# Coarse-level values from DRAM copies, zeros stored early, a float32r mask and a new weave in a one-core mixer layer

## Chip, cores and metric

The kernel runs on one core of one Trainium2 chip. The metric is device time in microseconds (us) of one execution. The core's engines are TensorE (PE for its matmuls, PEld for its weight loads), VectorE (DVE), ScalarE (ACT), GpSimd (POOL) and SyncE (SP, which here only issues transfers). Each engine takes its instructions in a fixed order; they wait for each other by semaphores.

## The reference

One layer on 512 tokens of width 1024, in float32: a norm, one projection to 3112 columns, three mixers on slices of it, and one output projection with a residual.

```python
h = rmsnorm(x, norm_g[l]);  proj = jnp.matmul(h, w_in[l])
(gq, gk, gv, glr, gg, su, sg, nq, nkv, ngl, ng) = jnp.split(proj, IN_SPLITS, axis=-1)
y_gla = gla_mixer(gq, gk, gv, glr, gg, ...)   # 4 heads, decayed causal attention, state 32 x 64
y_s5  = s5_mixer(su, sg, ...)                 # 16 groups, complex diagonal recurrence, 64 states each
y_nsa = nsa_mixer(nq, nkv, ngl, ng, ...)      # 8 heads: compressed, block and window attention
x = x + jnp.matmul(jnp.concatenate([y_gla, y_s5, y_nsa], -1), w_out[l])
```

What of it bears on the change:

- In GLA the score of a query i and a key j <= i carries a decay for each channel between them. The kernel computes it in levels of 64, 32, 16, 8, 4, 2 and 1 tokens: at the level of size s, queries in an odd block of s tokens meet the keys and values of the even block just before it. So a level needs the values of every second block of s tokens.
- S5 is computed in chunks of 8 tokens. Within a chunk the output is the chunk's input times a block-Toeplitz matrix, whose other half is zero by causality.
- The two attention branches of NSA that remain (with 8 blocks and the 16 best chosen, every visible block is taken) are causal attention over 512 tokens, with a mask on the diagonal tile.

## The kernel before

**Arithmetic.** Most projections split both factors into a high and a low part of type float32r and add three products. `mm` (line 165) issues every matmul that is not a transpose, so most matmuls have that line and are told apart by their tiles. `load_part` (lines 228 to 230) brings a quarter of a weight group from DRAM on SP (`wr`), rounds it on ACT (`wh`) and subtracts on DVE (`wl`). `proj_t` and `proj_n` are the projections that use them.

**Streams.** The work is written as five streams: `p` (projections: values, compressed blocks, then the groups nq0, kv1, kv2, ng0, nq1, gg, sg, ng1), `g` (GLA: constants, decay, state, levels, output norm), `s` (S5: parameters, input matrix, scan, output matrix, output, gating), `n` (NSA: a small network on compressed blocks, then attention for two groups of heads) and `o` (output projection). Each stream is a chain of generators that yield between steps. `ORDER`, a string of 355 letters, says which stream takes its next step; `weave` walks it. A letter whose stream still waits for another one's stage does nothing. What a step emits comes behind everything emitted before it. That emission order is the instructions' priority; the tile framework's planner, which keeps a timeline of its own, turns it into the order of each engine's queue, and may put a later step's instructions ahead where it takes the earlier one's as not ready. Weight loads and the evacuation of projections are raised by a fixed priority.

**Memory.** Tiles come from slots in size classes (`al`, `fr`); a tile that takes over a slot waits for the last user of the tile before it. For a tile that a transfer fills, that wait is SP's or POOL's, and all later transfers of that queue stand behind it. Matmul outputs go to 8 banks handed out the same way.

**The places that the change touches.**

- `gla_v` ends with the store of the values `vv` to a DRAM tile `vd` (line 394, on POOL). In `gla_intra` each level reads its rows back as `ve`, 128 partitions by 2 halves by 256, with one SP transfer for each half (lines 501 to 505), and `smk` times `ve` is the level's output.
- `s5_out_weights` computes the Toeplitz matrix's columns `kt` (lines 716 to 723: a transpose of `kx` on PE, the diagonal `dk`, one addition). It clears a tile `zz` on POOL and sends it to the first 7 of 15 rows of a DRAM tile `kd`, sends `kt` to the other 8, and reads the matrix `tt` back with overlapping rows (lines 725 to 732, all three transfers on POOL). `s5_y` multiplies `tt` with the chunk inputs `u`, in four token steps; in each, products of `xs` with `hb` come first, then those of `u` with `tt`.
- `cmp_mlp` loads its first weights in eight steps of two SP transfers of 256 KB (`w`, line 968) and multiplies each with `bk`.
- `attn_score` adds the causal mask to the diagonal tile by a matmul of a bf16 identity with a bf16 mask (line 1145), behind two float32r matmuls of the query and key parts.

Of the kernel before, what the change touches and what calls it, by code (L numbers as in the profile page):

```python
# [18 lines left out]
T = 512  # L19
# [16 lines left out]
for _n, _w in SMALL:  # L36
# [4 lines left out]
JOB = (("j3", 2048, 2), ("j4", 4096, 2))  # L41
WMAX = 280
ORDER = (
    "sspsssppppppsssssssssoopogggpggggggggggppnppppppppopgnsnggpnpnngppppppppgsgsssssgggggnppgsggsggggsnn"
    "sgsgngsggggsngggggggnnsssnppppppnnnnnnpnpnnnnpnppnggggggppppgggggggggggpnnngpppnpnnpnnppppnnnnnngppn"
    "pppnpppnnppppooopnnnnnnnnnnnnnnnnnnonnonnnnnnnnnnnnnnnoonnnnnnoopnonnnonnnnnnnnnooooononoonnnnononnn"
    "onnnnoooonnnnonnooonooooooonnoooooonoonnoonooonnnnnnnnn"
)
WARM = 13
RING = 6  # L50
# [11 lines left out]
def kernel(ctx: ExitStack, tc: tile.TileContext, a: dict, out: bass.AP):  # L62
# [101 lines left out]
    def mm(o, l, r, start, stop, **kw):  # L164
        PE.matmul(o, lhsT=l, rhs=r, start=start, stop=stop, **kw)  # L165

    ident = const.tile([128, 128], F32, name="ident")
    identb = const.tile([128, 128], BF16, name="identb")
    maskneg = const.tile([128, 128], BF16, name="maskneg")
    ng = const.tile([128, NK], F32, name="ng")  # L170
    small = const.tile([128, SM_W], F32, name="small")
    rsc = const.tile([128, NT], F32, name="rsc")
# [182 lines left out]
        nc.gpsimd.dma_start(out=u.rearrange("p g n -> p (g n)"), in_=ud.rearrange("j (c g) n -> (j c) (g n)", c=16))  # L355

    def consts():
        N["w2b"] = al("w2b", (17, 128), keep=True)
        N["dm"] = al("dm", (128, NLV - 1, 128), F32R, keep=True)
        N["dm0"] = al("dm0", (128, 128), F32R, keep=True)  # L360
        dmr = al("dmr", (128, NLV - 1, 128))
        dmr0 = al("dmr0", (128, 128))
        N["cmask"] = const.tile([128, 7, 64], F32, name="cmask")
        N["bmask"] = const.tile([128, 256], F32, name="bmask")
        N["hind"] = al("hind", (128, 4), keep=True)
        N["bones"] = const.tile([128, 128], F32, name="bones")
        N["eps"] = const.tile([128, 1], F32, name="eps")
        nb = al("nb", (128, 128))
        nc.sync.dma_start(out=dmr, in_=a["dm"][:, 1:])
        nc.sync.dma_start(out=dmr0, in_=a["dm"][:, 0])  # L370
        nc.sync.dma_start(out=N["w2b"], in_=a["w2b"])
        nc.sync.dma_start(out=N["hind"], in_=a["hind"])
        nc.sync.dma_start(out=N["cmask"], in_=a["cmask"])
        nc.sync.dma_start(out=N["bmask"], in_=a["bmask"])
        nc.sync.dma_start(out=N["bones"], in_=a["bones"])
        nc.sync.dma_start(out=nb, in_=a["maskneg"])
        G.memset(N["eps"], EPS)
        S.activation(N["dm"], dmr, AF.Copy)
        S.activation(N["dm0"], dmr0, AF.Copy)
        V.tensor_copy(identb, ident)  # L380
        V.tensor_copy(maskneg, nb)


    def gla_v():
        N["vv"] = vv = al("vv", (128, NT, 256), keep=True)
        lr = N["lr"]
        g = group("v")
        for i in range(NT):
            with scope():
                ps = yield from proj_n(g, i, 272)  # L390
                evac(vv[:, i], ps[:, :256], i)
                evac(lr[:, i], ps[:, 256:272], i)
        vd = dram.tile([T, 256], F32, name="vd")
        nc.gpsimd.dma_start(out=vd.rearrange("(i p) e -> p i e", p=128), in_=vv)
        N["vd"] = vd

    def gla_decay():
        lr, w2b, dm, qT, kT = N["lr"], N["w2b"], N["dm"], N["qT"], N["kT"]
# [89 lines left out]
    def gla_intra():  # L488
        oT, vd, qT, kT = N["oT"], N["vd"], N["qT"], N["kT"]
        for lo, lv in ((-1, (0,)), (0, (1, 2)), (2, (3, 4)), (4, (5, 6))):  # L490
            with scope():
                nl = len(lv)
                exp_ = yield from gla_exp(lo, nl)
                ves = []
                for x, l in enumerate(lv):
                    s = LEVELS[l]
                    ex = exp_[:, x].rearrange("p (b z a s) -> p z b a s", b=4, z=2, s=s)
                    for z, src in ((0, qT), (1, kT)):
                        sv = src.rearrange("p (b a two s) -> p two b a s", b=4, two=2, s=s)[:, 1 - z]
                        V.tensor_tensor(ex[:, z], ex[:, z], sv, op=OP.mult)  # L500
                    ve = al("ve", (128, 2, 256))
                    for q in range(2):
                        nc.sync.dma_start(out=ve[:, q], in_=vd[256 * q:256 * q + 256].rearrange(
                            "(a two r) e -> two a r e", two=2, r=s)[0])
                    ves.append(ve)
                yield
                for h in range(4):
                    with scope():
                        hs = slice(32 * h, 32 * h + 32)
                        pg = bank()  # L510
                        pv = pg[:, :nl * 128].rearrange("p (l q t) -> p l q t", l=nl, q=2)
                        for x in range(nl):
                            for i in range(NT):
                                ex = exp_[hs, x]
                                mm(pv[64 * (i % 2):64 * (i % 2) + 64, x, i // 2],
                                   ex[:, i * 128 + 64:i * 128 + 128], ex[:, i * 128:i * 128 + 64], True, True)
                        sm_ = al("smk", (128, nl, 2, 64))
                        V.tensor_tensor(sm_, pv, N["cmask"][:, lv[0]:lv[0] + nl, None, :].to_broadcast([128, nl, 2, 64]),
                                        op=OP.mult)
                        yield  # L520
                        e = slice(64 * (h % 2), 64 * (h % 2) + 64)
                        for x, l in enumerate(lv):
                            s = LEVELS[l]
                            for i in range(NT):
                                b = slice(64 * (i % 2), 64 * (i % 2) + 64)
                                o = oT[i % 2].rearrange("p (h q a two s) -> p h q two a s", h=2, q=2, two=2, s=s)
                                mm(o[e, h // 2, i // 2, 1], ves[x][b, i // 2, h * 64:h * 64 + 64],
                                   sm_[b, x, i // 2].rearrange("p (a s) -> p a s", s=s), False,
                                   l == 6 and h >= 2 and i >= 2)
                        yield  # L530
        drop("dm", "dm0", "Lh", "Ll", "qT", "kT")
# [141 lines left out]
    def s5_out_weights():  # L673
# [48 lines left out]
                        eyed[:, None, :].to_broadcast([128, 16, 16]), op=OP.mult)  # L722
        V.tensor_tensor(kt, pk[:, :256], dk.rearrange("p a b -> p (a b)"), op=OP.add)
        fr(pk)
        kd = dram.tile([15, 16, 256], F32, name="kd")
        zz = al("zz", (112, 256))
        G.memset(zz, 0.0)
        nc.gpsimd.dma_start(out=kd[0:7].rearrange("l c x -> (l c) x"), in_=zz)
        nc.gpsimd.dma_start(out=kd[7:15].rearrange("l c x -> (l c) x"), in_=kt)
        N["tt"] = tt = al("tt", (128, 8, 256), keep=True)  # L730
        ka = kd[:]
# [399 lines left out]
    def attn_score(gx, i, pr, brs):  # L1131
        kA = N["kA"][gx]
        n, nb, b0 = (i + 1) * 128, len(brs), brs[0]
        h = gx * 4 + 2 * pr
        q = [N[f"qA{gx}"][:, 2 * pr + e, tok(i)] for e in range(2)]
        dn = al("dn2", (128, 2, nb), keep=True)
        p = al("p", (128, 2, T), keep=True)
        pv = p[:, :, :nb * n].rearrange("p e (b t) -> p e b t", b=nb)
        with scope():
            nm = al("nm", (128, 2, nb))  # L1140
            sv = [bank("ps")[:, :nb * n].rearrange("p (b t) -> p b t", b=nb) for _ in range(2)]
            for e in range(2):
                mm(sv[e], q[e], kA[:, 0, b0:b0 + nb, :n], True, False)
                mm(sv[e], q[e], kA[:, 1, b0:b0 + nb, :n], False, False)
                mm(sv[e][:, :, n - 128:], identb, maskneg[:, None, :].to_broadcast([128, nb, 128]), False, True)
            for e in range(2):
                V.tensor_reduce(nm[:, e], sv[e], axis=AX.X, op=OP.max, negate=True)  # L1147
            for e in range(2):
                for b in range(nb):
                    S.activation(pv[:, e, b], sv[e][:, b], AF.Exp, bias=nm[:, e, b:b + 1], accum_out=dn[:, e, b:b + 1])  # L1150
        V.reciprocal(dn, dn)
        V.tensor_tensor(dn, dn, gates[:, i].rearrange("p (h b) -> p h b", b=3)[:, h:h + 2, 1 + b0:1 + b0 + nb], op=OP.mult)  # L1152
        G.tensor_tensor(pv, pv, dn[:, :, :, None].to_broadcast([128, 2, nb, n]), op=OP.mult)  # L1153
        fr(dn)
        return p
# [66 lines left out]
def _prepare(inp):  # L1222
# [66 lines left out]
    a["bones"] = (t[:, None] // 64 == t[None, :] // 64).astype(np.float32) / 64.0  # L1289
    a["bmask"] = (t[:, None] // 32 == np.arange(256)[None, :] // 64).astype(np.float32)  # L1290
    a["hind"] = (t[:, None] // 32 == np.arange(4)[None, :]).astype(np.float32)
    a["eyed"] = (t[:, None] == np.arange(16)[None, :]).astype(np.float32)
    tok = np.arange(T).reshape(NT, 128).T
    vis = (np.arange(32) * 16 + 31)[None, None, :] <= tok[:, :, None]
# [30 lines left out]
```

## Time and profile before

| | |
|---|---|
| three runs | 377.41 us median, 374.65 to 380.54 |
| the profiled execution's own time | 376.93 us |
| its span, first to last instruction | 375.0 us |
| granted TensorE clock, mean over the span | 0.958 |
| TensorE busy with matmuls | 350.9 us (94%) |
| VectorE, ScalarE, GpSimd busy | 241.7, 163.7, 74.4 us |
| HBM traffic | 33.31 MB read, 3.39 MB written |

A row of the profile with busy times gives an engine's busy time and its instruction count. The row of the granted clock gives tenths of 2.4 GHz; the two levels are 2.4 GHz (1.0) and 1.2 GHz (0.5). Ends of matmuls are modelled and neighbours overlap, so the distance from start to start says more about a matmul's price than its duration. A wait is the idle time of an engine ahead of an instruction, with what ended it.

### The profile page before, as it was taken

The page shows a single profiled execution, that of the slowest core. Times are in us where ns is not written, and L with a number is a line of the kernel's source. Part 1 is how long each engine was busy: PE and PEld are TensorE (multiplying, and loading weights), DVE is VectorE, ACT ScalarE, POOL GpSimd, SP SyncE. Part 2 cuts the span into 40 slices and gives each one's busy share as a digit, 9 for nine tenths or more (in the row PEclk, how much of TensorE's full clock was granted, in tenths as well). Part 3 has the DMA queues.
Part 4 walks back from the last instruction along what each step waited for, and adds up shares of the span by engine and source line. Part 5 has one row for each costly group of instructions (what it writes and reads, how often), then busy time and mean ns, then how long its engine had stood idle before and what let it go on. Part 6 is the DMA issues. An engine that isn't in the chain of part 4 may idle for free.

```text
span 375.0 us, 6778 instructions
## 1 busy us (share of the span) xinstructions
PE 350.9 (94%) x2620; PEld 277.7 (74%) x2620; DVE 241.7 (64%) x502; ACT 163.7 (44%) x355; POOL 74.4 (20%) x75
## 2 busy tenths in 40 slices
PE   7999997999995995999999999899989997999996
PEld 3889977999884663679877867687666885677785
DVE  2749979985995220356674876985898776564332
ACT  3773441447743010353532436844876254632110
POOL 0000420100010000000130122463576243541000
PEclk9999998999999576999999999999999998799999
DMA  6995563344258023651324020020332024110022
GB/s 188 318 353 164 133 207 92 93 142 138 61 152 281 14 73 88 227 144 33 101 77 142 12 47 0 3 59 28 113 114 86 0 73 152 56 59 2 34 94 97
DMA packets 26509, 39.81 MB, mean 106 GB/s; under 512 B 2981, under 2 KB 15534, under 8 KB 26478
## 3 DMA queue, kind: packets, MB, share of 16 engines
q1 hardware_dynamic: 25150, 35.94, 31.7%
q0 software_dynamic: 1328, 3.46, 3.1%
q8 instruction: 20, 0.33, 0.4%
q14 instruction: 11, 0.09, 0.1%
HBM read 33.31 MB, written 3.39 MB: 98 GB/s over the span
## 4 chain that ended last, share of the span: by engine, by line
PE 65%; DVE 14%; DMA 11%; ACT 5%; issue 3%; POOL 1%; SPq 0%; ACTq 0%; DVEq 0%; POOLq 0%
PE pp L165 28%; PE pt L165 17%; PE ps L165 14%; PE pt L1172 4%; DMA w<-in_w_dram 2%; DMA tt<-kd 2%; DMA wor<-in_w_out_dram 2%; DVE wl L230 2%; DMA xr<-in_xT_dram 1%; DMA dmr<-in_dm_dram 1%; DMA wr<-in_w_nq_dram 1%; DMA kd<-kt 1%; DVE wol L1076 1%; ACT wh L229 1%; DVE nm L1147 1%
## 5 line engine op out<-in xcount | busy, mean ns | idle before, releaser
L165 PE MATMUL pp<-wl,xh 128*128 128x256 f32 (+2 forms) x160 | 46.3, 291 | 2.4 <-DVE wl L230 2.4
L230 DVE TENSOR_TENSOR wl<-wr,wh 128x512 fp32r<-128x512 f32 (+2 forms) x48 | 35.0, 741 | 20.6 <-ACT wh L229 18.9
L1153 POOL TENSOR_TENSOR p<-p,dn 128x1024 f32<-128x1024 f32 (+2 forms) x24 | 39.4, 1640 | 44.6 <-DVE dn L1152 30.5
L165 PE MATMUL pp<-wh,xh 128*128 128x256 f32 (+2 forms) x160 | 46.4, 292 | 0.6 <-ACT qr L280 0.6
L165 PE MATMUL pp<-wh,xl 128*128 128x256 f32 (+2 forms) x160 | 46.5, 292 | 0.0
L229 ACT ACTIVATE wh<-wr 128x512 fp32r<-128x512 f32 (+2 forms) x48 | 30.2, 635 | 29.4 <-PE pp L165 12.5
L1150 ACT ACTIVATE p<-ps,nm 128x512 f32<-128x512 f32 (+3 forms) x64 | 33.1, 528 | 16.5 <-DVE nm L1147 14.7
L165 PEld LDWEIGHTS pp<-wl,xh 128*128 128x128 f32 x160 | 30.8, 193 | 2.9 <-DVE wl L230 2.6
L165 PE MATMUL pp<-xh,wh 128*128 128x512 f32 x80 | 32.1, 401 | 0.6 <-DVE sgt L285 0.6
L1147 DVE TENSOR_REDUCE nm<-ps 128x1 f32<-128x512 f32 (+3 forms) x48 | 27.8, 593 | 7.4 <-PE ps L165 7.3
L165 PEld LDWEIGHTS pp<-wh,xh 128*128 128x128 f32 x160 | 30.8, 193 | 1.9 <-ACT qr L280 0.8
L165 PE MATMUL pp<-xl,wh 128*128 128x512 f32 x80 | 31.8, 398 | 0.0
L165 PE MATMUL ps<-kA,qA 128*128 128x512 f32 (+2 forms) x96 | 29.8, 405 | 2.0 <-ACT p L1150 1.2
L165 PE MATMUL pp<-xh,wl 128*128 128x512 f32 x80 | 31.6, 398 | 0.0
L165 PEld LDWEIGHTS pp<-wh,xl 128*128 128x128 f32 x160 | 30.8, 193 | 1.0 <-issue 0.8
L165 PE MATMUL pt<-pT,kvr 128*64 128x128 f32 x320 | 28.0, 288 | 2.2 <-DVE pT L1176 2.2
L1172 PE MATMUL pt<-ident,p 128*128 128x128 f32 x160 | 25.3, 287 | 0.5 <-POOL p L1153 0.5
L165 PEld LDWEIGHTS pt<-pT,kvr 128*64 128x64 f32 x320 | 19.8, 140 | 7.2 <-DVE pT L1176 2.6
L1172 PEld LDWEIGHTS pt<-ident,p 128*128 128x128 f32 x160 | 17.8, 143 | 5.8 <-issue 4.3
L1178 ACT ACTIVATE pT<-pt 128x512 f32<-128x512 f32 (+1 forms) x22 | 12.3, 560 | 18.5 <-PE pt L1172 18.4
L165 PEld LDWEIGHTS ps<-kA,qA 128*128 128x128 f32 x96 | 15.6, 197 | 4.8 <-ACT p L1150 1.7
L165 PEld LDWEIGHTS pp<-xh,wh 128*128 128x128 f32 x80 | 15.1, 188 | 3.9 <-DVE sgt L285 0.8
(381 smaller groups left out, 760.5 us busy)
## 6 DMA issues: line engine op xcount, KB each, us to landing
w<-in_w_dram SPq DMA_DIRECT2D x16, 256.0 KB, 4.5
wor<-in_w_out_dram SPq DMA_DIRECT2D x16, 256.0 KB, 2.8
xr<-in_xT_dram SPq DMA_DIRECT2D x8, 256.0 KB, 5.0
xn<-in_xn_dram SPq DMA_DIRECT2D x4, 512.0 KB, 8.3
wr<-in_w_kv_dram SPq DMA_DIRECT2D x8, 256.0 KB, 3.3
wr<-in_w_nq_dram SPq DMA_DIRECT2D x8, 256.0 KB
wr<-in_w_ng_dram SPq DMA_DIRECT2D x8, 256.0 KB, 3.7
opart<-in_xn_dram SPq DMA_DIRECT2D x4, 512.0 KB
```

The source lines that it names most:

```text
L165: PE.matmul(o, lhsT=l, rhs=r, start=start, stop=stop, **kw)
L229: S.activation(hs[qt][:, :, :w], r[:, :, :w], AF.Copy)
L230: V.tensor_tensor(ls[qt][:, :, :w], r[:, :, :w], hs[qt][:, :, :w].bitcast(F32), op=OP.subtract)
L1076: (V if hf else G).tensor_tensor(wol[k][:, c], r, woh[k][:, c].bitcast(F32), op=OP.subtract)
L1147: V.tensor_reduce(nm[:, e], sv[e], axis=AX.X, op=OP.max, negate=True)
L1150: S.activation(pv[:, e, b], sv[e][:, b], AF.Exp, bias=nm[:, e, b:b + 1], accum_out=dn[:, e, b:b + 1])
L1153: G.tensor_tensor(pv, pv, dn[:, :, :, None].to_broadcast([128, 2, nb, n]), op=OP.mult)
L1172: PE.transpose(pb[:, tok(x_)], p[:, e, c:c + 128], ident)
L1178: S.activation(pt[:, :w], pb[:, :w], AF.Copy)
```

## The change

Four edits:

- **Values.** Behind the store of `vd` come three further stores on POOL: one that writes the even blocks of 64 tokens to a DRAM tile of half the size, two that do so for blocks of 32. The levels of 64 and 32 then read `ve` in one SP transfer each; the level of 1 is also written as one transfer, from `vd`. The other four keep two.
- **Zeros.** `kd` is made in `consts`, and its first 7 rows are filled there by a transfer from a DRAM input of zeros. `zz`, its clearing and its transfer in `s5_out_weights` go.
- **Mask.** The identity and the mask for `attn_score` become float32r instead of bf16, in the same 48 matmuls.
- **Weave.** `ORDER` is another string of 355 letters, with differences nearly everywhere.

Where the two strings put some steps, found by walking them (letters counted from 0):

| step | before | after |
|---|---|---|
| `s5_params`, first step | 0 | 1 |
| store of the values | 28 | 28 |
| `w1` loads and products 0 to 4 of `cmp_mlp` | 53, 55, 59, 61, 62 | 54, 56, 59, 60, 61 |
| `kt`, `kd` and the load of `tt` | 54 | 55 |
| `ve` of the level of 64 | 72 | 71 |
| four token steps of `s5_y` | 73, 75, 76, 77 | 69, 70, 72, 73 |
| `w1` 5 to 7 | 85, 98, 99 | 82, 104, 105 |
| projection kv1 | 65 to 86 | 68 to 92 |
| projection kv2 | 126 to 140 | 94 to 147 |
| projection ng0 | 147 to 158 | 156 to 165 |
| projection nq1 | 159 to 186 | 166 to 189 |

```diff
-    identb = const.tile([128, 128], BF16, name="identb")
-    maskneg = const.tile([128, 128], BF16, name="maskneg")
+    identr = const.tile([128, 128], F32R, name="identr")
+    maskneg = const.tile([128, 128], F32R, name="maskneg")
...
     def consts():
+        N["kd"] = kd = dram.tile([15, 16, 256], F32, name="kd")
+        nc.gpsimd.dma_start(out=kd[0:7].rearrange("l c x -> (l c) x"), in_=a["zero"])
...
-        N["vd"] = vd
+        N["vd"] = {0: vd}
+        for s in (64, 32):
+            N["vd"][s] = half = dram.tile([T // 2, 256], F32, name=f"vd{s}")
+            hv = half.rearrange("(i h r) e -> h r i e", i=NT, r=s)
+            for h in range(64 // s):
+                nc.gpsimd.dma_start(out=hv[h], in_=vv[2 * s * h:2 * s * h + s])
...
-                    for q in range(2):
-                        nc.sync.dma_start(out=ve[:, q], in_=vd[256 * q:256 * q + 256].rearrange(
-                            "(a two r) e -> two a r e", two=2, r=s)[0])
+                    if s in vd:
+                        nc.sync.dma_start(out=ve, in_=vd[s].rearrange("(q p) e -> p q e", q=2))
+                    elif s == 1:
+                        nc.sync.dma_start(out=ve, in_=vd[0].rearrange("(q p two) e -> two p q e", q=2, two=2)[0])
+                    else:
+                        for q in range(2):
+                            nc.sync.dma_start(out=ve[:, q], in_=vd[0][256 * q:256 * q + 256].rearrange(
+                                "(a two r) e -> two a r e", two=2, r=s)[0])
...
-        kd = dram.tile([15, 16, 256], F32, name="kd")
-        zz = al("zz", (112, 256))
-        G.memset(zz, 0.0)
-        nc.gpsimd.dma_start(out=kd[0:7].rearrange("l c x -> (l c) x"), in_=zz)
+        kd = N["kd"]
...
-                mm(sv[e][:, :, n - 128:], identb, maskneg[:, None, :].to_broadcast([128, nb, 128]), False, True)
+                mm(sv[e][:, :, n - 128:], identr, maskneg[:, None, :].to_broadcast([128, nb, 128]), False, True)
```

## Rows read from the trace of the kernel before

**Rows 1.** The page's busy totals, its 40 slices of the span for TensorE, and the granted clock by slice.

```profile
PE 350.9 (94%) x2620; PEld 277.7 (74%) x2620; DVE 241.7 (64%) x502; ACT 163.7 (44%) x355; POOL 74.4 (20%) x75
...
PE   7999997999995995999999999899989997999996
...
PEclk9999998999999576999999999999999998799999
```

**Rows 2.** The longest waits of TensorE: what waited, for what, us in total, times, the longest.

```profile
PE ps L165 <- DMA tt<-kd: 4.4, 1, 4.4
PE pt L165 <- DMA w<-in_w_dram: 4.3, 1, 4.3
```

**Rows 3.** Busy time of each engine in chosen stretches: stretch, its length, busy us and instructions of PE, PEld, DVE, ACT and POOL, granted clock, share of the DMA engines' time, GB/s.

```profile
66.00:117.60 51.60, 50.84 (x443) 47.05 (x441) 44.85 (x98) 29.63 (x53) 3.13 (x6) 1.00 0.44 130
...
121.56:135.21 13.65, 13.16 (x64) 9.06 (x66) 3.24 (x8) 0.60 (x1) 0.00 (x0) 0.50 0.04 15
135.21:142.04 6.83, 5.51 (x52) 3.92 (x48) 1.57 (x3) 1.78 (x3) 0.00 (x0) 1.00 0.56 153
...
142.04:148.86 6.82, 3.84 (x17) 2.20 (x19) 0.00 (x0) 0.00 (x0) 0.00 (x0) 0.50 0.24 60
150.00:230.00 80.00, 79.19 (x807) 60.73 (x804) 51.15 (x106) 31.30 (x57) 10.91 (x13) 1.00 0.33 92
230.00:316.00 86.00, 81.24 (x594) 61.00 (x592) 66.77 (x122) 52.22 (x135) 41.67 (x28) 1.00 0.21 62
```

**Rows 4.** The order of POOL's instructions from 40 to 120 us: start, us, line, operation, out<-in, count, and in brackets the idle time before and what ended it.

```profile
44.13 0.76 POOL L394 DMA_DIRECT2D vd<-vv  x1
52.71 2.11 POOL L949 DMA_DIRECT2D aT<-tm  x4 [7.82 <-DVE fr L635]
...
107.89 0.31 POOL L727 MEMSET zz<- 112x256 f32 x1 [41.12 <-DVE Ll L191]
108.50 0.57 POOL L728 DMA_DIRECT2D kd<-zz  x1 [0.30 <-POOL zz L727]
109.06 0.57 POOL L729 DMA_DIRECT2D kd<-kt  x1
114.43 0.92 POOL L732 DMA_DIRECT2D tt<-kd  x1 [4.80 <-DMA kd<-kt]
```

**Rows 5.** From VectorE's order in time, the instruction that makes `kt`; and, from the instructions on the tile `kx`, the transposes that `kt` reads (duration ns min/median/max, first and last start).

```profile
108.35 0.42 DVE L723 TENSOR_TENSOR kt<-ps,dk 128x256 f32<-128x256 f32 x1
...
L716 PE MATMUL ps<-ident,kx x2: 273/301/329, 96.5 to 96.7; 128*128 128x128 f32 x2
```

**Rows 6.** TensorE's matmuls in order of time around the two waits.

```profile
115.65 0.39 PE L165 MATMUL pp<-xh,wl 128*128 128x512 f32 x1
...
122.05 0.69 PE L165 MATMUL ps<-tt,u 128*64 128x128 f32 x4 [4.44 <-DMA tt<-kd]
...
145.02 1.11 PE L165 MATMUL pt<-w,bk 128*64 128x256 f32 x2 [4.30 <-DMA w<-in_w_dram]
...
159.59 0.28 PE L165 MATMUL pp<-wh,xh 128*128 128x256 f32 x1
159.71 0.28 PE L165 MATMUL pp<-wl,xh 128*128 128x256 f32 x1
```

**Rows 7.** SP's transfers in order of time between 115 and 151 us, and what SP waited longest for ahead of a `ve` transfer.

```profile
117.70 0.41 SPq L228 DMA_DIRECT2D wr<-in_w_sg_dram  x1
134.50 1.19 SPq L503 DMA_DIRECT2D ve<-vd  x2
135.86 2.63 SPq L968 DMA_DIRECT2D w<-in_w_dram  x2
...
SPq L503 <- PE pt L165: 19.8, 3, 16.3
```

**Rows 8.** Transfers: count, KB of each, median us from issue to landing.

```profile
tt<-kd POOLq DMA_DIRECT2D x1, 1024.0 KB, 7.6
...
aT<-tm POOLq DMA_DIRECT2D x8, 64.0 KB, 2.0
...
kd<-kt POOLq DMA_DIRECT2D x1, 128.0 KB, 4.8
```

**Rows 9.** The mask among its neighbours: TensorE's matmuls and weight loads in order of time.

```profile
280.83 0.63 PE L165 MATMUL ps<-kA,qA 128*128 128x512 f32 x2
...
281.30 0.10 PEld L165 LDWEIGHTS <-identb 128*128 128x128 bf16 x1 [0.27 <-issue]
281.30 0.23 PE L165 MATMUL ps<-maskneg,identb 128*128 128x128 bf16 x1
...
281.34 0.71 PE L165 MATMUL ps<-kA,qA 128*128 128x512 f32 x2
...
281.90 0.23 PE L165 MATMUL ps<-maskneg,identb 128*128 128x128 bf16 x1
```

**Rows 10.** Weight loads by form: count, busy us, mean ns, idle before and what ended it.

```profile
L165 PEld LDWEIGHTS ps<-kA,qA 128*128 128x128 f32 x96 | 15.6, 197 | 4.8 <-ACT p L1150 1.7 <-issue 1.2 <-DVE kA L923 0.9
...
L165 PEld LDWEIGHTS <-identb 128*128 128x128 bf16 x48 | 4.7, 98 | 9.9 <-issue 9.4
```

**Rows 11.** Two float32r matmuls on 128 columns that follow each other, in a stretch where the clock was 0.5.

```profile
128.00 0.42 PE L165 MATMUL ps<-dm,Ll 128*128 128x128 f32 x1
128.21 0.41 PE L165 MATMUL ps<-dm,Lh 128*128 128x128 f32 x1
```

More of the change, by code (lines that the diff above doesn't have):

```diff
@@ L43 @@
 ORDER = (
[L44 to L47, printed above, removed]
+    "psssssssppspsposspssposggpogpoopoognpgpppgggppppggggggnsnggnnngppppppssgssgsgpgppsnspppgggggppppsggg"
+    "gggsnnsgsngsggggsngpgggsnnnnnnnnnnnsgsggpppnnnpppgggggggpggpnnppgppppppgggggggnpnngnnnnpnppnppppnnnn"
+    "nnnnpppppppgpnnppnnnnnpnnnnnnnnnnnnnnnnnnonnonnnnnnnonnnnoooonnooonnnnnopoooonnnooonnnnnoonnnnnnnnnn"
+    "nnnnnonnnoooooonononnoooonoonooononnonoonoononnnnnonnon"
 )
@@ L379, in consts @@
         S.activation(N["dm0"], dmr0, AF.Copy)
-        V.tensor_copy(identb, ident)
+        V.tensor_copy(identr, ident)
         V.tensor_copy(maskneg, nb)
@@ L1291, in _prepare @@
     a["hind"] = (t[:, None] // 32 == np.arange(4)[None, :]).astype(np.float32)
+    a["zero"] = np.zeros((112, 256), np.float32)
     a["eyed"] = (t[:, None] == np.arange(16)[None, :]).astype(np.float32)
```

## The prediction, made before the change was run

> **What bounds the kernel now.** I read the page's totals first: TensorE is busy for 350.9 of 375.0 us, and no other engine comes near [rows 1]. So a change can win only TensorE's own work, its idle time (some 24 us) and the time that it runs at the half clock. The slices show where these lie: ones of 5 to 7 tenths in the clock's row stand at about 120 to 150 us, and the busy row dips there too [rows 1]. Then the waits of TensorE: the two longest are one of 4.4 us for the transfer of `tt` and one of 4.3 us for the first weights `w` of `cmp_mlp`; no other reaches 2.5 us [rows 2].
>
> Then the stretches. From 66 to 117.6 us TensorE is busy for 50.84 of 51.6 us at the full clock, with VectorE at 44.85. Behind the first wait the clock is 0.5 from 121.56 to 135.21 us, with 13.16 us of matmuls, and behind the second from 142.04 to 148.86 with 3.84 us [rows 3]. Work at half clock takes twice as long, so half of those matmul times is lost: 6.6 and 1.9 us. The bill of the two waits is 4.4 + 6.6 + 4.3 + 1.9 = 17.2 us. After 150 us little is left: 0.8 us idle in 150 to 230 and 4.8 in 230 to 316 [rows 3].
>
> Why do the waits stand there? `kt` is added at 108.35 us, its transfer is issued at 109.06, the load of `tt` at 114.43 after a wait of 4.80 for that transfer [rows 4, 5], and TensorE goes on at 122.05 [rows 6]. That is 13.3 us from the end of `kt` (108.77) to its use. In the meantime TensorE used up the projection ng0 until 115.65 us; the next projection in its queue is nq1 at 159.59 [rows 6]. So the queue's own order leaves nothing to cover the end of the chain. The second wait is SP's doing: after 117.70 it issues nothing until 134.50, where it was held 16.3 us by TensorE for a `ve` transfer, and two loads of `w` stand behind that at 135.86 [rows 7].
>
> **The change part by part**, against the profiled execution's 376.93 us (span 375.0 and 1.9 around it; the median of the runs is 0.5 above).
>
> *Zeros.* The clearing of `zz` (107.89) and its transfer (108.50) go; they kept POOL until 109.06, and `kt` was ready at 108.77 [rows 4, 5]. That is 0.3 us on the chain to `tt`, from the rows. The transfer of `kt` (128 KB) landed in 4.8 us beside the zeros; the nearest one alone, `aT` with 64 KB, in 2.0 [rows 8]. So the gain is between nothing (the chain is covered anyway) and 0.3 + 2.8 = 3.1 us; I take 0.5, near the issue time, because the load of `tt` itself (1 MB, 7.6 us) is unchanged. The early transfer of zeros costs nothing: POOL, busy for 20% of the span [rows 1], stands idle most of the time, and 112 KB are some 0.3% of what is read. Without that cover it would be one issue of 0.57 us on POOL [rows 4]. The Trainium skill ("DMA: Bandwidth & Descriptors", Anatomy of one DMA) gives a transfer on this path a fixed 2 us and bytes over 436 GB/s, so an estimate of 2.3 us for `kt` against the row's 4.8; by that rule the chain would be 2.5 us shorter and the sum lower by as much.
>
> *Values.* SP issues 11 `ve` transfers instead of 14. SP's issue takes 0.6 us of each (1.19 for two [rows 7]), 1.8 us in all, and TensorE never waited for `ve` among its longest waits [rows 2]; cover is SP's idle time, so nothing on the path. The three further stores stand on POOL behind 44.13 at 0.76 each, 2.3 us; behind them on POOL are the `aT` transfers, which wait for VectorE until 52.71 [rows 4], so they are covered by that idle time of 7.8 us. Without it, the compressed blocks would come 2.3 us later.
>
> *Mask.* Two pairs of the same matmuls tell its price: the first pair starts at 280.83, its mask at 281.30, so 0.47 for two; from the mask to the next pair is 0.04, and that pair takes until 281.90, so 0.56 for two. One mask matmul costs 0.04 + 0.09 = 0.13 us [rows 9]: the load of the bf16 identity begins only when the matmuls before it have run (48 loads, 9.4 us of such idle time [rows 10]). In float32r at 128 columns the nearest row is 0.21 us from start to start at clock 0.5, so about 0.105 at 1.0 [rows 11]. That is 0.02 less each, 1.0 us for 48. The ends: half the 0.12 of a 256-column one [rows 6], so 0.07 less each, a gain of 3.4 us; or the longer load shows in full, 197 against 98 ns [rows 10], a loss of 4.8 us. I take the gain of 1.0, as float32r loads before the 512-column matmuls are hidden already.
> A rule speaks against this edit. The Trainium skill ("TensorE: Matmul & The Clock Gate", Weight-path perf modes) says that the fast weight load needs 128 weights that aren't FP32. The trace agrees on the load (98 against 197 ns); by the rule alone the 4.8 us would be lost.
>
> *Weave.* The direct edits come to 1.5 us; the rest hangs on the new order. The letters decide little by themselves: ng0 has letters 147 to 158 and ran before `s5_y` with 73. So I weigh what the new walk does to the two waits. For `tt`: between the `kt` step and the first token step of `s5_y` stood 9 half projections, now 5. Each is 12 matmuls of 0.12 us [rows 6], so 5.8 us less by the letters: the first wait is not helped. For `w`: the `ve` load of the level of 64 stood ahead of all four token steps of `s5_y`, with TensorE's wait among them; now two of them and the same five `w` loads stand ahead of it, so SP is less likely to hold `w` behind a slot that TensorE frees late. And projections kv1 and kv2 now have letters behind `s5_y`. I take it that the second wait goes with its clock, 4.3 + 1.9 = 6.2 us, and that the first stays. Ends: 17.2 us (both go) and nothing, or a loss (below).
>
> Sum: 376.9 - 0.5 - 1.0 - 6.2 = 369.2 on the profiled scale, 369.7 beside the median.
>
> **Rivals.**
> - *Neither wait goes.* The planner put TensorE's work in an order of its own, and SP still stands in line for `ve`. Then only the direct 1.5 us are left: 375.9. For it: both waits come from transfers that landed later than the queue's order allowed for, and the letters around them moved by few places. Against: the string differs nearly everywhere.
> - *Both go.* Were `kt` added earlier, `tt` would be there at 117.6: the transposes it reads were done at 97 us, 11 us before it [rows 5], so there is room for the 4.4. Then 376.9 - 1.5 - 17.2 = 358.2, or 358.7 beside the median. Against: VectorE was busy up to there [rows 3], and the change does nothing to its work.
> - *Slower: the cover before `tt` shrinks.* If the 5.8 us fewer of projections show in full, TensorE waits 10.2 us for `tt`, and the stretch from 135.21 to 142.04 (5.51 us of matmuls [rows 3]) runs at half clock too, 5.5 us more; the second wait is absorbed in part. 376.9 - 1.5 + 5.8 + 5.5 = 386.7, less some 2 of the second wait: 385. It decides once more than about 1.5 us of the cover is lost without the `w` wait going. For it: the letters. Against: TensorE had no cover left from 115.65 on in any case.
> - *The mask's load shows.* A loss of 4.8 where I have a gain of 1.0: 369.7 + 5.8 = 375.5. Against: the idle time of 9.4 us ahead of the bf16 loads [rows 10], which float32r loads don't have.
>
> **How the numbers follow.** The second wait goes: 0.34, between 365 and 374 with the ends of the mask and of the zeros. Neither goes: 0.24. Both go: 0.20. Slower: 0.18. The mask's load: 0.04. A measurement of this kernel tells about 2% from no change, so faster means under 369.9. Faster: half of 0.34, and 0.20: 0.37. Slower by over 2% (above 385.0) would need all of the fourth case and it ends just there; as its price is rough and other places of the order can fail likewise, I keep 0.18. Within 2%: 0.17 + 0.24 + 0.04 = 0.45. The likeliest case gives 369.7, and its middle lies at the bound, so that "within" leads. The range goes from 359 (both) to 381: what lies above is the slower case, under 2 in 10.
>
> **What would show it.** The waits of TensorE: `w` gone from them, `tt` still at 3 to 5 us, with a clock of 0.5 for one stretch instead of two between 115 and 150 us. In SP's order no gap of 16 us ahead of `ve`. For the zeros: no clearing at POOL, and `kt`'s transfer right behind the addition. For the mask: idle time ahead of the identity's loads well under 9.4 us, and about 0.1 us from a mask to the next start. It is wrong if TensorE's longest wait is a new one, after 150 us above all, or if `kt` is added at another time than 108 us by more than 3 us: then the order of VectorE moved and my sum misses its main term.

## The result, and the profile after the change

The changed kernel takes 363.64 us (median of 4 runs, 361.91 to 364.86) where the kernel before takes 377.35 (374.65 to 380.54): a ratio of 0.966, 95% interval 0.959 to 0.973. The forecast was 369.7 within 359 to 381; "faster", which came, had a chance of 0.37 there, behind 0.45 for "within 2%". Some runs of a kernel are slower than its others by some per cent, so medians here are over every run and ratios over the faster ones alone, of which two kernels below had too few.

The page after, beside [rows 1]: busy totals, TensorE's slices and the granted clock.

```profile
PE 342.8 (95%) x2620; PEld 279.9 (77%) x2620; DVE 238.4 (66%) x502; ACT 163.4 (45%) x355; POOL 77.2 (21%) x77
...
PE   6999997979999599999999999899999999899996
...
PEclk9899999989999858999999999999999999999999
```

The dip at 120 to 150 us is shorter, and the 7 and 8 that stood near the end of the clock's row are gone. TensorE's longest waits after, beside [rows 2]:

```profile
PE ps L165 <- DMA tt<-kd: 4.0, 1, 4.0
PE pp L165 <- DVE wl L230: 3.8, 2, 2.7
PE pt L165 <- ACT xh L296: 2.2, 1, 2.2
PE pt L165 <- DVE pT L1185: 1.9, 3, 1.0
```

The wait on `w` is gone, the one on `tt` is there, and none other is above 3 us in one piece. The stretches after, beside [rows 3]; the columns are the same:

```profile
66.00:121.20 55.20, 52.51 (x447) 48.97 (x445) 45.97 (x102) 28.65 (x51) 3.54 (x6) 0.97 0.42 124
121.20:125.42 4.22, 0.21 (x4) 0.00 (x0) 0.00 (x0) 0.00 (x0) 0.00 (x0) 0.84 0.77 251
124.04:137.69 13.65, 12.27 (x60) 8.53 (x60) 3.21 (x7) 1.82 (x3) 0.00 (x0) 0.50 0.13 42
137.69:150.00 12.31, 12.31 (x105) 8.11 (x104) 2.75 (x5) 2.25 (x4) 0.00 (x0) 1.00 0.73 216
150.00:230.00 80.00, 79.06 (x827) 62.73 (x825) 53.73 (x112) 37.80 (x69) 11.25 (x13) 1.00 0.28 77
230.00:318.00 88.00, 85.61 (x638) 68.78 (x638) 70.06 (x138) 53.21 (x151) 50.29 (x33) 1.00 0.27 79
```

Of the two half-clock stretches in this part the one behind the `tt` wait is left (12.27 us of matmuls, 13.16 before); from 137.69 us TensorE is busy without a gap at the full clock. POOL's order after, beside [rows 4]:

```profile
46.61 1.74 POOL L402 DMA_DIRECT2D vd<-vv  x3
56.88 2.11 POOL L958 DMA_DIRECT2D aT<-tm  x4 [8.54 <-DVE tm L953]
...
112.46 0.56 POOL L738 DMA_DIRECT2D kd<-kt  x1 [44.12 <-DVE on L558]
116.67 0.91 POOL L741 DMA_DIRECT2D tt<-kd  x1 [3.65 <-DVE nfs L187]
```

The copies cost POOL 1.74 us, covered by its 8.54 us of idle time. The zeros are gone from the chain. `kt` is now added at 111.74 us and the first product of `tt` starts at 125.42, so the chain takes 13.68 us; it took 13.70 [rows 5, 6]. SP's order after, beside [rows 7]:

```profile
127.19 0.37 SPq L228 DMA_DIRECT2D wr<-in_w_sg_dram  x1
137.87 0.37 SPq L510 DMA_DIRECT2D ve<-vd  x1
138.83 0.81 SPq L977 DMA_DIRECT2D w<-in_w_dram  x2
140.79 0.33 SPq L971 DMA_DIRECT2D w<-in_w2c_dram  x1
```

SP is still held for 10 us ahead of `ve`, and `w` still stands behind it. But two `w` transfers are issued in 0.81 us, not 2.63. That small row is the trail that the experiments follow.

### The profile page after: what moved, and what is told of

The parts are those of the page before. It is cut to its first block, busy times and chain, and to the rows that moved or that the text cites. A ratio compares the mean times of both kernels' runs of the same rounds, so it can differ in the third digit from the quotient of the medians.

```text
span 361.8 us, 6782 instructions
## 1 busy us (share of the span) xinstructions
PE 342.8 (95%) x2620; PEld 279.9 (77%) x2620; DVE 238.4 (66%) x502; ACT 163.4 (45%) x355; POOL 77.2 (21%) x77
## 4 chain that ended last, share of the span: by engine, by line
PE 54%; DVE 5%; DMA 4%; ACT 4%; issue 1%; ACTq 0%
PE pp L165 25%; PE pt L165 14%; PE ps L165 10%; PE pt L1181 4%; DMA tt<-kd 2%; DMA wor<-in_w_out_dram 2%; DVE nm L1156 1%; ACT p L1159 1%; DVE wol L1085 1%; ACT woh L1084 1%; ACT pT L1187 1%; DVE dn L1161 1%; DVE pT L1185 0%; DVE mixf L574 0%; DVE sgt L288 0%
## 5 line engine op out<-in xcount | busy, mean ns | idle before, releaser
L165 PE MATMUL ps<-kA,qA 128*128 128x512 f32 (+2 forms) x96 | 28.5, 389 | 1.1 <-ACT p L1159 1.1
L165 PE MATMUL pt<-pT,kvr 128*64 128x128 f32 x320 | 26.6, 281 | 1.9 <-DVE pT L1185 1.9
L1181 PE MATMUL pt<-ident,p 128*128 128x128 f32 x160 | 24.4, 280 | 0.0
```

Of the source, the lines that this page charges most:

```text
L1181: PE.transpose(pb[:, tok(x_)], p[:, e, c:c + 128], ident)
```

## The experiments

**Each part alone.** Three kernels: the mask edit alone, the new ORDER alone, and the other edits with the old ORDER.

```diff
# mask_alone: before, with
-    identb = const.tile([128, 128], BF16, name="identb")
-    maskneg = const.tile([128, 128], BF16, name="maskneg")
+    identr = const.tile([128, 128], F32R, name="identr")
+    maskneg = const.tile([128, 128], F32R, name="maskneg")
# weave_alone: before, with the changed kernel's ORDER
# edits_no_weave: the changed kernel, with the ORDER of before
```

> The kernel before with the float32r mask alone. First theory (the weave carries the gain, the direct edits little): about 1.0 us less than before, 376.4; both long waits of TensorE (tt 4.4, w 4.3 us) still there, since only the 48 mask matmuls change. Rival (TensorE's own work, which is 4.3 us shorter after the change, is shortened by the mask): 373. Third (the longer float32r load shows in full): 382.

> The kernel before with the new string of letters alone. First theory (the weave carries the gain): the wait for w and its stretch at half clock are gone, the wait for tt of about 4 us stays; 363.6 plus the 1.5 us of the direct edits, 365. Rival (the direct edits free SP and POOL, and the string only fits to them): 372 to 377, with the wait for w still at 4 us.

> The changed kernel with the old string: values, zeros and mask alone. First theory: 375.9, that is before less 1.5, with both long waits. Rival (the direct edits carry it): 365, with the wait for w gone.

Measured, against 376.22 us of before on the same chip: mask alone 377.15, ratio 1.004 (0.999 to 1.009); weave alone 372.03, 0.987 (0.980 to 0.995); the edits without the weave 370.08, 0.982 (0.973 to 0.991). The product of the last two is 0.970, inside the interval of the whole. But the parts did not do what I had given them. The weave alone keeps both waits; its longest:

```profile
PE ps L165 <- DMA tt<-kd: 5.0, 1, 5.0
PE pt L165 <- DMA w<-in_w_dram: 3.8, 1, 3.8
```

and with the old weave and the edits the `w` wait is gone:

```profile
PE ps L165 <- DMA tt<-kd: 3.3, 1, 3.3
PE pp L165 <- DVE wl L230: 3.3, 2, 2.8
```

**Why `w` was late.** A closer look at the kernel before, first three stretches (same columns), then its transfers issued from 134 to 138.2 us (KB each, median us to landing):

```profile
136.30:137.90 1.60, 1.60 (x19) 1.48 (x18) 0.55 (x1) 0.59 (x1) 0.00 (x0) 1.00 0.15 44
138.20:141.00 2.80, 2.52 (x24) 1.64 (x24) 0.69 (x1) 1.06 (x2) 0.00 (x0) 1.00 0.79 240
143.50:146.50 3.00, 1.48 (x6) 0.73 (x7) 0.00 (x0) 0.00 (x0) 0.00 (x0) 0.50 0.14 45
```

```profile
w<-in_w_dram SPq DMA_DIRECT2D x2, 256.0 KB, 8.6
ve<-vd SPq DMA_DIRECT2D x2, 128.0 KB
```

While `ve` alone is under way, the DMA engines are busy for 0.15 of their time, as much as 2.4 of the 16, and move 44 GB/s; then, with what is queued behind it, 240. Around the end of TensorE's wait for `w` (145.02 us [rows 6]) they are back at 0.14 and 45 GB/s. The old `ve` load of the coarsest level takes 2 blocks of 64 rows out of `vd`, so the outermost step of its source has the length 2. The Trainium skill ("DMA: Bandwidth & Descriptors", Why a DMA increments its semaphore by 16 and not by 1) says that a transfer is spread over the largest number of engines, up to 16, that divides the outermost lengths of both its sides: 2 here, which the share of 0.15 is near, and 16 for the copy. The theory: such a narrow transfer holds up what is queued behind it. Four kernels test it.

```diff
# values_alone: before, with the copies and the ve loads from them, and the level of 1 in one transfer
# zeros_alone: before, with the zero half of kd written at the start
# after_old_values: the changed kernel, with the values as before
# blocks_split: before, with
+                        sq = vd[256 * q:256 * q + 256].rearrange("(a two r) e -> two a r e", two=2, r=s)[0]
+                        if s in (64, 32):
+                            for ai in range(128 // s):
+                                nc.sync.dma_start(out=ve[ai * s:ai * s + s, q], in_=sq[ai])
```

> The kernel before with one edit, the values of the two coarsest levels loaded from the copies of their rows. Theory (shape of the transfer): in the kernel before, the two ve loads of the coarsest level and the two w loads right behind them on SP are slow (the w landings 8.6 us beside a median of 4.7), and the edits without the weave, in which ve is one transfer over whole rows, have w landings of at most 5.1 us and no w wait. If this edit alone is the reason, the longest wait on w (4.3 us) and the second half-clock stretch go, the wait on tt stays at 3 to 5 us, and the time is 376.2 - 4.3 - 1.9 = 370 us (367 to 373). Rival (the zero half): clearing the buffer early frees its slot, which shifts the planner's work; then this edit alone changes nothing: 376.2 us (374 to 379) with a w wait of 4 us.

> The kernel before with one edit, the zero half of S5's matrix written at the start from an input instead of from a cleared buffer just ahead of kt. Theory (shape of the ve transfers): the w wait of about 4.3 us stays, with w landings of 8 to 9 us, since the ve loads are the old ones; the wait on tt shortens by at most 0.5 us, and the time is 375.7 us (373 to 378). Rival (the freed slot and POOL's shorter queue do it): the w wait goes and the time is 370 us (367 to 373).

> The changed kernel without one edit: the values of the coarsest levels are loaded from vd in blocks, as in the kernel before; new weave, early zeros and the float32r mask stay. Theory (shape of the ve transfers): two ve transfers of the coarsest level stand ahead of two w loads again, w lands in 8 to 9 us, TensorE waits 3 to 4 us on it, and the time is near that of the weave alone, 372 us less at most 1 for zeros and mask: 371.5 us (369 to 374). Rival (zeros are what removed the wait): 364 us (362 to 367), no w wait.

> The kernel before, but each ve load of the two coarsest levels is issued block by block: 4 transfers of 64 rows for the coarsest level and 8 of 32 rows for the next, instead of 2 and 2, with the same rows read and no copies. Theory (the shape of a transfer, a few blocks as its outermost step, makes it and what is queued behind it slow): each small transfer is over rows only, so the w loads behind it land in at most 6 us, the w wait goes as with the copies, and the time is 370 us plus up to 1 us for 8 more issues on SP: 370 to 372. Rival (the number of transfers or SP's issue time ahead of w is what makes w late): 2 more issues ahead of the w loads make it later, the w wait grows to 5 us or more, and the time is 377 us (375 to 380).

Against 377.43 us of before: values alone 371.35, ratio 0.976 (0.971 to 0.982); the changed kernel with the old values 370.48, 0.982 (0.977 to 0.987); blocks split 372.22, 0.979 (0.971 to 0.987). Zeros alone: 375.42 to 390.21, no ratio; its profile has the `w` wait (4.0 us) and a `w` landing of 8.8. In values_alone TensorE waits 0.8 us for `w` at most; the stretch of the `ve` transfer, then the landings (issued 133 to 135 us):

```profile
134.30:135.30 1.00, 1.00 (x10) 1.00 (x10) 0.00 (x0) 0.24 (x1) 0.00 (x0) 1.00 0.82 259
```

```profile
w<-in_w_dram SPq DMA_DIRECT2D x2, 256.0 KB, 5.0
ve<-vd SPq DMA_DIRECT2D x1, 256.0 KB, 2.5
```

The same rows now move at 259 GB/s. In blocks_split no copy exists and SP has more to issue, and yet `w` is on time and the wait on it gone (SP's order, then the transfers from 136 to 138.5 us):

```profile
136.04 1.16 SPq L506 DMA_DIRECT2D ve<-vd  x2
137.89 0.82 SPq L972 DMA_DIRECT2D w<-in_w_dram  x2
```

```profile
w<-in_w_dram SPq DMA_DIRECT2D x2, 256.0 KB, 3.7
ve<-vd SPq DMA_DIRECT2D x2, 64.0 KB, 2.3
```

And with the old values in the changed kernel `w` lands in 8.4 us and the wait is back:

```profile
PE ps L165 <- DMA tt<-kd: 4.9, 1, 4.9
PE pp L165 <- DVE wl L230: 3.1, 2, 2.8
PE pt L165 <- DMA w<-in_w_dram: 3.1, 1, 3.1
```

The shape of the transfer is the cause, not the zeros, the number of issues or the copies as such.

**Which level, and which resource.**

```diff
# blocks_split_64: as blocks_split, with
-                        if s in (64, 32):
+                        if s == 64:
# ve_from_pool: before, with
-                        nc.sync.dma_start(out=ve[:, q], in_=vd[256 * q:256 * q + 256].rearrange(
+                        nc.gpsimd.dma_start(out=ve[:, q], in_=vd[256 * q:256 * q + 256].rearrange(
```

> The kernel before, with the ve loads of the coarsest level alone issued block by block (4 transfers of 64 rows instead of 2); the next level stays as it was. Theory: the loads ahead of the late w are those of the coarsest level, so this edit alone is enough: w lands in at most 6 us, no w wait over 1.5 us at the place, time 370.5 us (368 to 373). Rival (both levels are needed, or the gain with all blocks split came from another order of the work): the w wait stays above 3 us and the time is 375 to 378 us.

> The kernel before, with all ve loads issued by POOL instead of SP, in their old blocks. Two theories of why the w loads behind ve are slow. Shared engines: the two ve transfers run on few of the 16 DMA engines (in 136.3 to 137.9 us of the kernel before the DMA share is 0.15) and a w transfer, spread over all, ends when its part on those few ends; then the queue that issues ve doesn't matter, and if the ve and w loads still fall together, w lands in about 8 us and TensorE waits 3 to 4 us on it: 376 us (373 to 379). SP's queue: w stands behind ve in the same queue; then w lands in 3 to 5 us, the w wait goes, and the time is 370 us (367 to 373). The split has a hole: POOL may issue ve at another moment than SP did, so the landing of w is to be read beside the time at which ve was issued.

The coarsest level alone is enough: 370.73 us against 377.45, ratio 0.984 (0.975 to 0.993), `w` landing in 3.9 us and no wait on it among the longest. From POOL, 381.65 us (374.82 to 383.89), no ratio; its time tells the two theories apart no further. Its transfers issued from 139 to 141.5 us:

```profile
w<-in_w_dram SPq DMA_DIRECT2D x2, 256.0 KB, 6.4
ve<-vd POOLq DMA_DIRECT2D x2, 128.0 KB, 8.3
```

SP issues its two `w` in 0.83 us again, so their slow issue came of the narrow transfers ahead in SP's own queue. But `w` still lands in 6.4 us, between the 3.7 and the 8.6, and the waits on it come to 2.5 us; the narrow transfers themselves take 8.3. The run changes more than the queue, though: POOL's `ve` went in packets of 4 KB, SP's in packets of 1 KB.

The trace of the kernel before settles more. It keeps the landing of a `w` as 16 updates of a semaphore (no view prints them). Of the first `w`, 14 come by 140.11 us and the last two at 144.86 and 144.98, right behind the last two of the second `ve` (144.23 and 144.45); TensorE goes on at 145.02. In blocks_split all 16 of that `w` come between 140.17 and 141.44. So 14 of the 16 parts passed the narrow transfers, and two waited 4.9 us: that is the theory of shared engines, while SP's queue as a whole would have held all 16. From POOL, too, the last two parts of the second `w` are late (148.28 and 148.51, the other 14 by 145.17), beside a `ve` that lands at 149.24, but by 3.3 us; what the other queue changes, one run does not settle.

**The `tt` wait.** What `kt` reads is there some 11 us before its addition [rows 5]. With a tile of its own and a raised priority it can be added earlier.

```diff
# kt_early_after: the changed kernel, with
-        kt = al("kt", (128, 256))
-        eyed = al("eyed", (128, 16))
+        kt = const.tile([128, 256], F32, name="kt")
+        eyed = const.tile([128, 16], F32, name="eyed")
...
-        dk = al("dk", (128, 16, 16))
+        dk = const.tile([128, 16, 16], F32, name="dk")
+        with tc.high_priority(offset=BOOST):
...
# kt_early_before: before, with the same
# kt_early_lean: the changed kernel, with kt and eyed alone, no dk:
+        V.tensor_tensor(kt.rearrange("p (a b) -> p a b", a=16), sm("s5d")[:, :, None].to_broadcast([128, 16, 16]),
+                        eyed[:, None, :].to_broadcast([128, 16, 16]), op=OP.mult)
+        with tc.high_priority(offset=BOOST):
+            V.tensor_tensor(kt, pk[:, :256], kt, op=OP.add)
```

> The changed kernel, in which kt, dk and eyed have places of their own instead of slots handed on, and the two instructions that make dk and kt are raised in priority. Theory (kt is late because its operand dk waits for a slot in VectorE's queue; its transposes were done 11 us earlier): kt comes at about 102 us instead of 111.7, tt lands at about 115, before TensorE needs it; the wait of 4.0 us and the 6.1 us lost at half clock go: 363.6 - 10.1 = 353.5. Rival 1 (the stretch from 120 to 138 us is small dependent matmuls that keep the half clock anyway): only the wait goes, 359.6. Rival 2 (the planner moves the product with tt forward by as much, and the wait stays): 363.

> The kernel before with the same move of kt as in the run kt_early_after (kt, dk and eyed in tiles of their own, their two additions raised), all else as it was. Theory (the two waits have causes of their own): the tt wait goes, the w wait of about 4 us stays, and the gain is the one that the move brought to the changed kernel, 2.8 us of the medians: 373.5 us (371 to 376). Rival (the w wait is a follower of the tt wait, since S5's late start pushes what fills TensorE): both waits go and the time is 366 us (362 to 369).

> The changed kernel with kt early as in kt_early_after, but with one 1 KB tile of its own in place of two: the eyed product is written into kt early, and only the final addition is raised. In kt_early_after two new waits of 3.5 us (on tm) and 2.4 us (on kvr) took back part of the gain; tm stood behind four 1.22 us instructions of VectorE's chain (L705 and L706). Theory (these waits come of the raised dk and the smaller arena): they go, the tt wait stays away, and the time is 360.8 - 4 = 357 us (354 to 360). Rival (with S5 early, another of VectorE's chains comes due together with tm in any order): as kt_early_after, 361 us (359 to 363), with at least one wait over 2 us ahead of 100 us.

kt_early_after: 360.84 us against 376.22, ratio 0.957 (0.950 to 0.964); `kt` is added at 94.78 us, the `tt` wait and its half clock are gone. kt_early_before: 371.63 against 377.45, 0.987 (0.978 to 0.996), no `tt` wait, but the `w` wait still 3.7 us. So the two waits have causes of their own, as expected. But the move brought the changed kernel less than expected, since two new waits take its place ahead of 100 us in kt_early_after:

```profile
PE pp L165 <- DVE tm L954: 3.5, 1, 3.5
PE pp L165 <- ACT kvr L280: 2.4, 1, 2.4
```

kt_early_lean is the fastest: 358.21 (357.85 to 362.20) against 377.45, ratio 0.953 (0.945 to 0.961). My reason for it fell, though; in its profile, which is of the slowest of its five runs, both new waits are there:

```profile
PE pp L165 <- DVE tm L953: 4.1, 1, 4.1
PE pp L165 <- ACT kvr L280: 2.5, 1, 2.5
```

So neither the raised `dk` nor its 1 KB makes them; `tm` stands on VectorE behind four instructions of 1.22 us (L705, L706), and that order came with the early `kt` both times. What makes lean faster than kt_early_after, if it is, stays open: they ran in different sets, and the intervals of their ratios overlap.

## Why the prediction came out as it did

The time lay inside the range, which is 22 us wide, and 6 us below the forecast: the gain is 13.7 us, the sum had 7.7. The two waits did as foretold, `w` went and `tt` stayed, but the first for another reason than mine, so that part came true by luck. The step that failed is the ascription: "I take it that the second wait goes with its clock" was put on the weave, and the values were priced at nothing.

- **Values: forecast 0, measured 6.7 to 11.1 us** (377.43 times one less the interval of the ratio; 6.1 by the medians). The `w` wait and its half clock had cost 6.2 us. In values_alone's profile the half clock behind the `tt` wait is shorter as well, with 6.00 us of matmuls where it had 13.16, a loss of 3.0 us instead of 6.6; why, I did not trace. The failed sentence is "cover is SP's idle time, so nothing on the path". I counted what the `ve` issues cost SP, 1.8 us, and not what the transfers do to those queued behind them. The sign stood in the rows: two `w` took 2.63 us of SP where two `ve` took 1.19 [rows 7]. I took it for the ordinary price of a larger transfer. A `w` elsewhere would have shown that it isn't: four of them take 1.83 us at 148.68 in the same trace. Nor was it the slot for which SP is held, "The second wait is SP's doing": blocks_split issues its `ve` at 136.04 us, later than the 134.50 of before, and values_alone holds SP nearly as long as before, both without a long wait on `w`:

```profile
SPq L508 <- PE pt L165: 16.5, 2, 13.8
```

- **Weave: forecast 6.2 us from the `w` wait, measured 4.8** (0.0127 of 376.22; 2.0 to 7.6 by the interval), but elsewhere. "SP is less likely to hold `w`" did not come true: with the weave alone TensorE waits 3.8 us for `w`. Here is the part of the span from 150 us on, first for before and weave_alone, then for edits_no_weave and the changed kernel:

```profile
150.00:375.00 225.00, 215.91 (x1720) 164.42 (x1716) 144.00 (x276) 99.86 (x241) 62.81 (x48) 0.98 0.24 73
```

```profile
150.00:368.20 218.20, 209.75 (x1711) 160.77 (x1707) 138.00 (x276) 99.83 (x241) 63.87 (x48) 1.00 0.25 73
```

```profile
150.00:367.60 217.60, 209.09 (x1666) 165.96 (x1660) 137.77 (x273) 98.16 (x239) 63.53 (x48) 0.99 0.24 68
```

```profile
150.00:361.80 211.80, 205.19 (x1697) 164.81 (x1695) 140.04 (x276) 98.76 (x241) 64.09 (x48) 1.00 0.24 72
```

The new weave takes 6.8 and 5.8 us off this part in these profiled runs (weave_alone's is the fastest of its four), with nearly the same number of matmuls left or more; 6.2 and 3.9 of it are TensorE's busy time. One piece can be seen. Before, TensorE waits once for 2.22 us on `pT`, and there the half clock sets in (TensorE's order, then the stretch):

```profile
316.44 0.69 PE L165 MATMUL pt<-pT,kvr 128*64 128x128 f32 x2 [2.22 <-DVE pT L1176]
```

```profile
316.10:322.90 6.80, 6.46 (x26) 3.98 (x26) 4.42 (x9) 4.11 (x12) 3.14 (x2) 0.50 0.48 152
```

Half of 6.46 is 3.2 us lost. After, that wait is split into three of at most 1.0 us, and this stretch is at the full clock; all five kernels with the new weave have the three short waits, and none a half clock there. But the long wait does not by itself bring the half clock: all nine kernels with the old weave have it (1.9 to 2.8 us), and in four of them, mask_alone, zeros_alone, blocks_split and kt_early_before, the clock does not fall there. So it is not shown that the weave saves these 3.2 us. My stretches in [rows 3] ended at 316 us, just ahead of it, though the page's row showed the 8 and the 7 [rows 1]; "After 150 us little is left" was wrong by some 3 us for that execution. The rest of the weave's gain I can't put in one place, and its cause stays open.
- **Zeros: forecast 0.5; no gain shows.** The clearing left the chain, `kt` landed in 3.9 us instead of 4.8 [rows 8], and `tt` took it back, 8.7 instead of 7.6: 13.68 us against 13.70. Nor did the zeros slow `kt`, as the 2.8 us at the forecast's upper end had it: in zeros_alone it lands in 4.8 us still, `tt` in 8.8, and TensorE waits 5.1 us for `tt`.
- **Mask: forecast a gain of 1.0; measured 0.3 gained to 3.2 lost** (376.22 times the interval's distance from 1). The idle time ahead of the identity's loads fell as I said, but the load is twice as long, 188 ns where it was 98 [rows 10]:

```profile
L165 PEld LDWEIGHTS ps<-maskneg,identr 128*128 128x128 f32 x48 | 9.0, 188 | 1.1
```

The one probably went against the other; no run parts them. The Trainium skill's rule ("TensorE: Matmul & The Clock Gate", Weight-path perf modes) is right as to the load; the full price of 4.8 us lies outside the interval.
- **`tt`: forecast to stay at 3 to 5 us; 4.0.** By my own mark the forecast was also wrong: `kt` moved by 3.4 us, more than the 3 I had allowed, so VectorE's order did move. The wait stayed, since TensorE's own work ahead of it grew by as much (it stopped at 121.4 us, not at 117.6). The rival in which the cover shrinks did not come about.
- **The rival that both go: forecast 358.7.** Taking the `tt` wait away as well gave 360.8 in kt_early_after: of the wait's 4.0 us and the 6.1 of half clock behind it (half of 12.27) the median kept 2.8 (363.64 less 360.84, from different sets) and the span 5.4.

## What to carry to other kernels

Price a transfer also by what stands behind it in its queue: a load whose outermost step is 2 long kept about 2 of 16 DMA engines busy here and cost about 6 us (by the ratio of blocks_split_64; 2.7 to 9.6 by its interval), though TensorE had no long wait for that load itself. When one transfer takes longer to issue than its like elsewhere in the same trace, look at the one ahead of it. And run each part of a change alone before you believe in the reason for the whole: here a total within its range stood on a wrong part.

## What the hardware showed that I had not expected

Two parts in 16 can decide when a transfer has landed: behind the narrow `ve` they came 4.9 and 4.0 us after the other 14 of the two `w`. And a narrow transfer slows the issuing, too: two `w` behind it on SP took 2.63 us to issue and 8.6 to land; behind the copy's transfer or the split blocks they took 0.81 to 0.82 us to issue and 3.7 to 5.5 to land. From another engine's queue, the narrow transfers no longer hold SP's issuing (0.83 us), but `w` still lands in 6.4 us.
